# Two-layer encoder on one core: the low parts of the queries stored at full height per head, and the on-chip buffers shared out anew

## The chip, the cores and the metric

One core of one Trainium2 chip. The metric is device time in microseconds, the median of several runs. The engines are named as in the profile: PE is TensorE (its weight loads stand as PEld), DVE is VectorE, ACT is ScalarE, POOL is GpSimd, SP is SyncE, which here only issues DMAs.

## The reference

Two layers. Each has a SwiGLU feed-forward block, a mixer and a second feed-forward block, each behind an RMS norm whose shift, scale and gate come from a conditioning vector `c`. The mixer sums three gated branches: attention A with a relative-position bias, pooling B, and attention C with forget gates. 512 tokens, 1024 features, 8 heads of 64 features in each attention. Cut to what matters here:

```python
mod = (silu(c) @ w_ada[l] + b_ada[l]).reshape(B, 9, 1024)
h = modulate(rms_norm(x, norm_gain[l, 0]), mod[:, 0], mod[:, 1])
x = x + 0.5 * mod[:, 2] * swiglu(h, ffn_w_gate[l, 0], ffn_w_up[l, 0], ffn_w_down[l, 0])
h = modulate(rms_norm(x, norm_gain[l, 1]), mod[:, 3], mod[:, 4])
x = x + mod[:, 5] * hybrid_mixer(h, ...)     # two attentions, each:
#   logits = rms_norm(q, gq) * 64**-0.5 @ rms_norm(k, gk).T + bias;  softmax;  @ v
h = modulate(rms_norm(x, norm_gain[l, 2]), mod[:, 6], mod[:, 7])
x = x + 0.5 * mod[:, 8] * swiglu(h, ffn_w_gate[l, 1], ffn_w_up[l, 1], ffn_w_down[l, 1])
```

## The kernel before

**Three passes a product.** Activations lie feature-major: 128 features on partitions, the 512 tokens on the free axis. Every float32 operand of a large product is split into a high and a low float32r part, and a product is three matmuls: high by high, high by low, low by high (`triple`, L118 to L120). A weight chunk is 512 KB: `wchunk` (L221) has SP load it into a tile `raw`, ACT writes the high part `whi` (L246), and DVE, or POOL in attention A and C, writes the low part `wlo` as `raw` minus `whi` (L248). One chunk feeds 24 matmuls of 512 columns. There are three tiles each of `raw`, `whi` and `wlo`.

**Modulation.** The 144 columns of `mod` are made on DVE, not on PE: a step (`mod_step`, L178) loads 512 KB of `w_ada` and one DVE instruction (L182) multiplies it by silu(c) and sums it, with a tiny read of the sum behind it. 16 steps stand in the start of the first block; the other 128 come from a queue, `MOD_RATE` = 0.8 steps for each weight chunk in a feed-forward block (L229). Their tiles are the same three `raw` tiles that the weights use, so weights and `w_ada` alternate in them.

**Who sets the order.** The source is written in one order, with tasks put off by a count of PE work (`later`, `poll`). A list scheduler then orders each engine's instructions once, at build time: an instruction may go ahead of one written earlier if the earlier one's inputs or its tile are not there yet in the scheduler's own reckoning. On the chip each engine takes its instructions in that fixed order.

**Norm between blocks.** The norm of the next block runs in two halves of 256 tokens while the last products of the block still run: DVE adds up the squares (L298), PE sums over features (L310), DVE takes 1/sqrt by three Newton steps of tiny instructions (L312 and L254 to L262) and scales a diagonal (L315), PE spreads it (L329), and DVE, POOL and ACT make eight pieces each of `hhi` and `hlo` (L338 to L343). The first three weight chunks of the next block go to tiles that attention uses (`ptb`, `pta`), so that they are ready before the norm.

**Logits.** `proj_qk` (L613) makes queries and keys, and `turn` puts them feature-major, two heads to 128 rows. For each head, `b[:, odd, :]` holds the high part in the head's own 64 rows; the other 64 rows hold, for the queries, the high part again, and for the keys the low part. So the first logits matmul (L746, 128 rows) gives high by high plus high by low. The low part of the queries lies in a tile `lows` shared by two pairs of heads, and the second matmul (L747) takes 64 rows of it against the 64 rows of the keys' high part. There are 4 query tiles for each of 8 heads, two attentions, two layers: 128 pairs of such matmuls, with 128, 256, 384 and 512 columns. Between the logits of one head stand turned weights (L769), products with V (L791, L792) and, as filler, the products of other branches.

Of the kernel before, what the change touches and what calls it, by code (L numbers as in the profile page):

```python
"""Two layers of a chunk-causal hybrid encoder (macaron SwiGLU, two attentions, pooling), one core.

Activations are held feature-major: features on partitions, the 512 tokens on the free axis.
Every float32 operand of a large product is split exactly into two float32r parts (12 bits each);
a product is three float32r passes: high*high + high*low + low*high.
"""
# [16 lines left out]
P = 128  # L23
T = 512
# [16 lines left out]
def encoder_kernel(tc, xT, c, w_ada, b_ada, gains, w_gate, w_up, w_down, w_qkv, w_f, w_ubg,  # L41
# [15 lines left out]
    uid = [0]  # L57

# [13 lines left out]
    def blk(tag, dt=F32R):  # L72
        bufs = {"xv": 4, "v2": 4, "b": 15}[tag]
        return st([P, 2, T], dt, tag, bufs)
# [53 lines left out]
    silc = [st([P, D], F32, "b", 15)]  # L128
    sil_dram = dr.tile([1, D], F32, name="sil_dram")
    crow = st([1, D], F32, "b", 15)  # L130
# [47 lines left out]
    def mod_step(l, j, d, tag="raw"):  # L178
        raw = st([P, D], F32, tag, 2 if tag != "raw" else 3)
        nc.sync.dma_start(raw, w_ada[l, j, d])  # L180
        m = modc[:, l, j, d:d + 1]
        nc.vector.tensor_tensor_reduce(out=raw, in0=raw, in1=silc[0], scale=1.0, scalar=badac[:, l, j, d:d + 1],  # L182
                                       op0=ALU.mult, op1=ALU.add, accum_out=m)
        s, kind = divmod(j, 3)
        if kind == 1:
            g = gainc[:, l, s, d:d + 1]
            return nc.vector.scalar_tensor_tensor(apre[:, l, s, d:d + 1], m, 1.0, g, op0=ALU.add, op1=ALU.mult).ins
        if kind == 2:
            nc.vector.tensor_scalar(m, m, 0.5, None, op0=ALU.mult)
# [4 lines left out]

    def mod_pop():
        if mod_ptr[0] < len(mod_queue):
            mod_step(*mod_queue[mod_ptr[0]])
            mod_ptr[0] += 1
# [5 lines left out]
    MOD_RATE = 0.8  # L204
# [7 lines left out]
    @contextlib.contextmanager  # L212
    def behind(engine):
        """What is issued here goes behind the last piece of the norm on that engine."""
        if engine in gate:
            with tc.issue_after(gate[engine]):
                yield
        else:
            yield

    def wchunk(src, shape, side=True, spare=None, lo_eng=None):  # L221
        if lo_eng is None:
            lo_share[1] += 1
            lo_eng = nc.gpsimd if lo_share[0] and lo_share[1] % lo_share[0] == 0 else nc.vector
        if quiet[0] > 0:
            quiet[0] -= 1
            if quiet[0] == 0:
                gate.clear()
        elif side and in_ffn[0]:  # L229
            mod_credit[0] += MOD_RATE  # L230
            while mod_credit[0] >= 1.0:
                mod_credit[0] -= 1.0
                mod_pop()
        raw = st([P] + list(shape), F32, "raw", 3)
        nc.sync.dma_start(raw, src)
        if spare == "ptb":
            both = st([P, 2] + list(shape), F32R, "ptb", 2)
            hi, lo = both[:, 0], both[:, 1]
        elif spare == "pta":
            hi = st([P] + list(shape), F32R, "pta", 2)  # L240
            lo = st([P] + list(shape), F32R, "pta", 2)
        else:
            hi = st([P] + list(shape), F32R, "whi", 3)
            lo = st([P] + list(shape), F32R, "wlo", 3)
        with behind("scalar"):
            nc.scalar.copy(hi, raw)  # L246
        with behind("vector"):
            lo_eng.tensor_tensor(lo, raw, hi.bitcast(F32), op=ALU.subtract)  # L248
        return hi, lo

# [21 lines left out]
    class Norm:  # L272
        """sq() takes in the finished tiles of x, front() and back() make one half of hhi/hlo."""
# [9 lines left out]
        def sq(self, d, hs):  # L283
            """hs: 0 or 1 for a half, None for all tokens."""
            cols = slice(0, T) if hs is None else slice(hs * HALF, (hs + 1) * HALF)
            x = xd(d)[:, cols]
            n = cols.stop - cols.start
            if d == 0:
                nc.scalar.activation(self.ssum[:, cols], x, AF.Square)
            elif d < KD - 1:  # L290
                q = t1(T)[:, :n]
                nc.scalar.activation(q, x, AF.Square)  # L292
                nc.gpsimd.tensor_tensor(self.ssum[:, cols], self.ssum[:, cols], q, op=ALU.add)  # L293
            else:
                self.work[hs] = st([P, 3 * HALF], F32, "strip", 2)
                w = self.work[hs][:, :HALF]
                nc.scalar.activation(w, x, AF.Square)
                nc.vector.tensor_tensor(w, w, self.ssum[:, cols], op=ALU.add)  # L298
            if d % 2 == 0 and self.xa[d // 2] is None:
                self.xa[d // 2] = blk(self.xtag, F32)  # L300
            nc.scalar.activation(self.xa[d // 2][:, d % 2, cols], x, AF.Identity, scale=apre[:, self.l, self.s, d:d + 1])  # L301
# [54 lines left out]
    def k_outer(chunk_src, nch, lhs_rhs, before_last=None):  # L356
        """chunk_src(c) -> AP of two K-tiles; lhs_rhs(hi, lo, ktile, j) -> operands of tile j.

        Yields (tile, half, sums) as they finish; the halves of the tokens come apart only with before_last."""
# [36 lines left out]
    def residual_tail(d, hs, acc_j, gate, nxt):  # L396
        """x += gate * product, and what the next norm takes from it."""
# [15 lines left out]
    class Ffn:  # L413
# [11 lines left out]
        def prefetch_weights(self):  # L425
            self.pre = [self.gate_up(0, 0, spare="ptb"), self.gate_up(1, 0, spare="ptb"), self.gate_up(0, 1, spare="pta")]
# [15 lines left out]
        def run(self, nxt):  # L442
            l, s, ms = self.l, self.s, self.ms
            in_ffn[0] = True
            for part, (f0, nf) in enumerate(((0, 12), (12, 10))):
# [33 lines left out]
                for c0 in (0, T):  # L479
# [9 lines left out]
                    if last and c0 == 0 and nxt is not None:  # L489
                        nxt.prefetch("v2")  # L490
                    split = last and c0 > 0
# [10 lines left out]
        def start(self):  # L502
            """The first three units while the modulation that they need still arrives."""
# [9 lines left out]
            with behind("vector"):  # L513
                mod_step(l, 0, 0, "ptb")
# [13 lines left out]
            with behind("vector"):  # L528
                ready = [mod_step(l, 1, 0, "pta")]
            gate.clear()  # L530

            def h(d):
# [6 lines left out]
                if d + 1 < KD:  # L539
                    with tc.issue_after(ready[0]):  # L540
                        mod_step(l, 0, d + 1, "ptb")
                    with tc.issue_after(scaled):
                        ready[0] = mod_step(l, 1, d + 1, "pta")
# [69 lines left out]
    def proj_qk(l, col, gcol, is_q, res, pre=None, norm=None):  # L613
# [22 lines left out]
        def turn(p):  # L636
# [4 lines left out]
            b = blk("b")  # L641
            first, second = slice(0, HD), slice(HD, P)
            for odd, (own, other) in enumerate(((first, second), (second, first))):
# [4 lines left out]
                if is_q:  # L648
                    nc.scalar.activation(low, pt[own, :], AF.Identity, scale=gc)
                    if p % 2 == 0 and odd == 0:  # L650
                        lows.append(blk("b"))
                    low = lows[p // 2][own, p % 2, :]
                nc.vector.scalar_tensor_tensor(low, pt[own, :], gc, dst[own, :].bitcast(F32),
                                               op0=ALU.mult, op1=ALU.subtract)
            res.append((b, lows[p // 2][:, p % 2, :]) if is_q else b)
# [20 lines left out]
    def finish_turns(upto=3):  # L676
        """The turned queries and keys of the head pairs up to this one are needed from here on."""
# [56 lines left out]
    def attention(qs, ks, vs, strip, ys, filler, budget, group):  # L734
        """All heads; per query tile: logits and softmax, later the turned weights, later the product with V.
        Between them goes other work for TensorE (filler)."""
        open_pt = {}

        def logits(h, i, strips):
            p, off = divmod(h, 2)  # L740
            rows = slice(off * HD, off * HD + HD)
# [5 lines left out]
            mm(s[:, :n], ql[rows, i * P:(i + 1) * P], k[rows, odd, :n], start=False, stop=True)  # L747
# [13 lines left out]
        def turn(h, i, pr):  # L761
            half, c = divmod(i, 2)
            nj = 2 * half + 2
            if c == 0:
                open_pt[h] = st([P, 2, nj, 256], F32R, "ptb" if half else "pta", 2)
# [55 lines left out]
    def pool_front(l, g):  # L821
# [5 lines left out]
        u = st([P, T + 16], F32, "pta", 2)  # L827
# [28 lines left out]
    def wpool_load(l):  # L856
        raw = st([P, 4, P], F32, "t1", 2)
        nc.sync.dma_start(raw, w_pool[l].rearrange("g c e -> c g e"))
        w = st([P, 2, 4, P], F32R, "pta", 2)
# [39 lines left out]
    class Mixer:  # L899
# [7 lines left out]
        def prefetch_weights(self):  # L907
            self.pre = [qkv_chunk(self.l, 0, c, spare=t) for c, t in enumerate(("ptb", "ptb", "pta"))]

        def run(self, nxt):  # L910
# [54 lines left out]
            if l + 1 < L:  # L965
                silc[0] = st([P, D], F32, "b", 15)
# [99 lines left out]
```

## Time and profile before

| | us |
|---|---|
| median of three runs | 2517.68 (2516.93 to 2517.75) |
| the profiled execution: span from first to last instruction | 2516.3 |
| PE busy | 2473.2 (98%) |
| DVE busy | 1373.3 (55%) |
| ACT busy | 981.1 (39%) |
| POOL busy | 361.9 (14%) |

For the profiled execution its span is the time that is known; the median of the runs is 1.4 us above it. The busy share of PE counts a matmul from its start to its modelled end, and neighbours overlap, so how dense PE works is read from the distance between the starts of matmuls, not from the share. The page also names the idle time in front of a group of instructions and what ended it; "issue" there means that the engine waited for nothing that the profile shows.

### The profile page before, as it was taken

To read this page: it belongs to the slowest core of one execution; us is meant where nothing else is said; L and a number is where in the kernel's file an instruction comes from. 1 tells how busy PE (TensorE), PEld (TensorE's weight loads), DVE (VectorE), ACT (ScalarE), POOL (GpSimd) and SP (SyncE) were. 2 spreads that over 40 slices of the span, in tenths; PEclk is the share of its full clock that TensorE was granted. 3 is DMA by queue.
4 is the path that set the end of the run, shared out by engine and by line. 5 is a ranking of instruction groups with operands and counts; after the bars stand their busy time and mean duration, and the time that the engine had idled before them with its cause. 6 is when DMAs were issued, how large, how long until landed. Compare 5 with 4: busy or idle time off the path is not lost. (4 is left out here: it accounts for less than half of the span.)

```text
span 2516.3 us, 30919 instructions
## 1 busy us (share of the span) xinstructions
PE 2473.2 (98%) x11898; PEld 2037.0 (81%) x11898; DVE 1373.3 (55%) x2429; ACT 981.1 (39%) x1632; POOL 361.9 (14%) x337
## 2 busy tenths in 40 slices
PE   6999999999999999999999999999999999999999
PEld 4888888766788898888888888977777888888888
DVE  8645546678753465555465555476777434533332
ACT  4322235666542352223342222356765323422231
POOL 2000002333322120000020000123232322100000
PEclk9999999999999999999999999999999999999999
DMA  7555543222323435545425554322132233223222
GB/s 247 199 175 176 178 158 101 83 72 86 113 83 105 151 101 173 178 168 176 143 101 175 169 182 154 131 91 82 54 108 97 89 110 133 76 93 100 98 95 84
DMA packets 116263, 320.02 MB, mean 127 GB/s; under 512 B 11122, under 2 KB 13298, under 8 KB 116116
## 3 DMA queue, kind: packets, MB, share of 16 engines
q1 hardware_dynamic: 116114, 318.05, 37.5%
q8 instruction: 93, 1.52, 0.2%
q14 instruction: 54, 0.44, 0.0%
q10 hardware_dynamic: 2, 0.00, 0.0%
HBM read 311.64 MB, written 6.38 MB: 126 GB/s over the span
## 5 line engine op out<-in xcount | busy, mean ns | idle before, releaser
L246 ACT CAST whi<-raw 128x1024 fp32r<-128x1024 f32 (+1 forms) x395 | 411.3, 1045 | 1058.0 <-PE acc L119 420.1
L248 DVE TENSOR_TENSOR wlo<-raw,whi 128x1024 fp32r<-128x1024 f32 x339 | 417.2, 1234 | 380.7 <-ACT whi L246 372.2
L118 PE MATMUL mm<-hhi,whi 128*128 128x512 f32 x1304 | 507.6, 389 | 0.0
L119 PE MATMUL mm<-hlo,whi 128*128 128x512 f32 x1304 | 507.3, 389 | 0.0
L120 PE MATMUL mm<-hhi,wlo 128*128 128x512 f32 x1304 | 507.3, 389 | 0.0
L118 PE MATMUL acc<-b,whi 128*128 128x512 f32 (+1 forms) x960 | 356.9, 372 | 0.0
L119 PE MATMUL acc<-b,whi 128*128 128x512 f32 (+1 forms) x960 | 353.8, 369 | 0.0
L120 PE MATMUL acc<-b,wlo 128*128 128x512 f32 (+1 forms) x960 | 353.7, 368 | 0.0
L182 DVE CUSTOM_DVE_ANT_0 raw<-raw,b,badac 128x1024 f32<-128x1024 f32 x128 | 164.4, 1284 | 254.4 <-DMA raw<-in_w_ada_dram 254.1
L118 PEld LDWEIGHTS mm<-hhi,whi 128*128 128x128 f32 x1304 | 245.0, 188 | 50.7
L120 PEld LDWEIGHTS mm<-hhi,wlo 128*128 128x128 f32 x1304 | 244.7, 188 | 51.0
L119 PEld LDWEIGHTS mm<-hlo,whi 128*128 128x128 f32 x1304 | 244.8, 188 | 50.8
L120 PEld LDWEIGHTS acc<-b,wlo 128*128 128x128 f32 x960 | 180.9, 188 | 30.3 <-issue 0.4
L119 PEld LDWEIGHTS acc<-b,whi 128*128 128x128 f32 x960 | 181.0, 189 | 30.0 <-issue 0.9
L118 PEld LDWEIGHTS acc<-b,whi 128*128 128x128 f32 x960 | 180.9, 188 | 30.1
L293 POOL TENSOR_TENSOR ssum<-ssum,t 128x256 f32<-128x256 f32 (+1 forms) x45 | 48.8, 1084 | 1070.7 <-ACT t L292 1070.7
L118 PE MATMUL acc<-hhi,whi 128*128 128x512 f32 x480 | 194.0, 405 | 3.2 <-ACT hhi L536 3.2
L120 PE MATMUL acc<-hhi,wlo 128*128 128x512 f32 x480 | 189.8, 395 | 3.0 <-POOL wlo L248 3.0
L119 PE MATMUL acc<-hlo,whi 128*128 128x512 f32 x480 | 188.9, 394 | 1.5 <-DVE hlo L538 1.5
L248 POOL TENSOR_TENSOR wlo<-raw,whi 128x1024 fp32r<-128x1024 f32 (+1 forms) x56 | 133.4, 2386 | 198.9 <-ACT whi L246 170.5
L118 PE MATMUL acc<-whi,hhi 128*128 128x512 f32 x336 | 144.5, 430 | 2.9 <-ACT t L623 2.5
L437 DVE TENSOR_TENSOR t<-mm,t 128x512 f32<-128x512 f32 x86 | 59.4, 691 | 137.9 <-PE mm L120 136.2
(234 smaller groups left out, 3569.5 us busy)
## 6 DMA issues: line engine op xcount, KB each, us to landing
raw<-in_w_ada_dram SPq DMA_DIRECT2D x128, 512.0 KB, 4.3
raw<-in_w_down_dram SPq DMA_DIRECT2D x88, 512.0 KB, 3.7
raw<-in_w_gate_dram SPq DMA_DIRECT2D x85, 512.0 KB, 3.6
raw<-in_w_up_dram SPq DMA_DIRECT2D x85, 512.0 KB, 3.5
raw<-in_w_ubg_dram SPq DMA_DIRECT2D x56, 512.0 KB, 3.5
raw<-in_w_qkv_dram SPq DMA_DIRECT2D x48, 512.0 KB, 3.6
raw<-in_w_branch_dram SPq DMA_DIRECT2D x24, 512.0 KB, 3.7
raw<-in_w_out_dram SPq DMA_DIRECT2D x16, 512.0 KB, 4.3
```

Source lines behind the costliest of these rows:

```text
L118: mm(o, lh, rh, start=start, stop=False)
L119: mm(o, lh, rl, start=False, stop=False)
L120: mm(o, ll, rh, start=False, stop=stop)
L182: nc.vector.tensor_tensor_reduce(out=raw, in0=raw, in1=silc[0], scale=1.0, scalar=badac[:, l, j, d:d + 1], op0=ALU.mult, op1=ALU.add, accu ...
L246: nc.scalar.copy(hi, raw)
L248: lo_eng.tensor_tensor(lo, raw, hi.bitcast(F32), op=ALU.subtract)
L293: nc.gpsimd.tensor_tensor(self.ssum[:, cols], self.ssum[:, cols], q, op=ALU.add)
L437: nc.vector.tensor_tensor(pr, pu, sg, op=ALU.mult)
```

## The change

The low parts of the queries get a tile per pair of heads, laid out per head: `lows[p][:, odd, :]` holds the low part in the head's own rows, and POOL writes zeros in the other 64. The second logits matmul then takes all 128 rows of it against all 128 rows of the keys' tile; what it adds is zero times the keys' low part. This needs two more 4 KB tiles per attention, and the tiles are shared out anew:

- `b` has 17 tiles instead of 15, `raw` 2 instead of 3, `pta` 1 instead of 2.
- the third prefetched weight chunk and the pooling branch's `u` move from `pta` to `b`.
- modulation steps use the four `v2` tiles (in attention C these hold the values) and no longer `raw`: in the start, and in every feed-forward block until the next block's norm needs `v2` (`mod_tag`). After that point a block issues no more steps. `MOD_RATE` goes from 0.8 to 1.0.

```diff
+    NB, NRAW = 17, 2
-        bufs = {"xv": 4, "v2": 4, "b": 15}[tag]
+        bufs = {"xv": 4, "v2": 4, "b": NB}[tag]
...
     def mod_step(l, j, d, tag="raw"):
-        raw = st([P, D], F32, tag, 2 if tag != "raw" else 3)
+        raw = st([P, D], F32, tag, {"v2": 4, "raw": NRAW}[tag])
...
-            mod_step(*mod_queue[mod_ptr[0]])
+            mod_step(*mod_queue[mod_ptr[0]], mod_tag[0])
...
-    MOD_RATE = 0.8
+    MOD_RATE = 1.0
...
-        elif side and in_ffn[0]:
+        elif side and in_ffn[0] and mod_tag[0] == "v2":
...
-        raw = st([P] + list(shape), F32, "raw", 3)
+        raw = st([P] + list(shape), F32, "raw", NRAW)
...
-        elif spare == "pta":
-            hi = st([P] + list(shape), F32R, "pta", 2)
-            lo = st([P] + list(shape), F32R, "pta", 2)
+        elif spare == "b":
+            hi = st([P] + list(shape), F32R, "b", NB)
+            lo = st([P] + list(shape), F32R, "b", NB)
...
             in_ffn[0] = True
+            mod_tag[0] = "v2"
...
                         nxt.prefetch("v2")
+                        mod_tag[0] = "raw"
...
             b = blk("b")
+            if is_q:
+                lows.append(blk("b"))
...
-                    if p % 2 == 0 and odd == 0:
-                        lows.append(blk("b"))
-                    low = lows[p // 2][own, p % 2, :]
+                    nc.gpsimd.memset(lows[p][other, odd, :].bitcast(F32), 0.0)
+                    low = lows[p][own, odd, :]
...
-            mm(s[:, :n], ql[rows, i * P:(i + 1) * P], k[rows, odd, :n], start=False, stop=True)
+            mm(s[:, :n], ql[:, odd, i * P:(i + 1) * P], k[:, odd, :n], start=False, stop=True)
...
-                open_pt[h] = st([P, 2, nj, 256], F32R, "ptb" if half else "pta", 2)
+                open_pt[h] = st([P, 2, nj, 256], F32R, "ptb" if half else "pta", 2 if half else 1)
...
-        u = st([P, T + 16], F32, "pta", 2)
+        u = st([P, T + 16], F32, "b", NB)
```

Because the steps have tiles of their own, the scheduler places them elsewhere. All line numbers of the changed kernel below are one to five higher than before for the same instruction.

First place, the DMA queue of SP in the first feed-forward block, behind the start. `raw` is a weight chunk or, before, a modulation step (`in_w_ada`). Before:

```order
L235 DMA raw_481<-in_w_gate_dram 128x1024
L180 DMA raw_487<-in_w_ada_dram 128x1024
L235 DMA raw_491<-in_w_up_dram 128x1024
L685 DMA wf_4694<-in_w_f_dram 128x64
L180 DMA raw_554<-in_w_ada_dram 128x1024
L235 DMA raw_558<-in_w_gate_dram 128x1024
L180 DMA raw_564<-in_w_ada_dram 128x1024
L235 DMA raw_568<-in_w_up_dram 128x1024
```

Here there are three steps for four weight chunks. Now, a few rows further on in the same block:

```order
L181 DMA v_117_635<-in_w_ada_dram 128x1024
L181 DMA v_121_645<-in_w_ada_dram 128x1024
L238 DMA raw_572<-in_w_up_dram 128x1024
L238 DMA raw_639<-in_w_gate_dram 128x1024
L181 DMA v_130_712<-in_w_ada_dram 128x1024
L181 DMA v_134_722<-in_w_ada_dram 128x1024
L238 DMA raw_649<-in_w_up_dram 128x1024
L238 DMA raw_716<-in_w_gate_dram 128x1024
L181 DMA v_143_789<-in_w_ada_dram 128x1024
L181 DMA v_147_798<-in_w_ada_dram 128x1024
```

From here on the steps settle at five for every two weight chunks until the 49 of the first block are through, by the 24th weight chunk behind the start; then the block has none. Before they were spread over the block and the mixer behind it.

Second place, DVE between the first mixer and the second feed-forward block, in the second half of the norm: from the sum of squares (`nt_v`) through the Newton steps to the first piece of `hlo`. Before:

```order
L343 SCALAR_TENSOR_TENSOR hlo<-b_7580,modc,hhi 128x256
L312 TENSOR_SCALAR nt_v_7784<-acc_7781 128x2
L254 TENSOR_SCALAR nt_j_7786<-nt_v_7784 128x2
L260 TENSOR_TENSOR nt_q_7788<-nt_j_7786 128x2
L261 SCALAR_TENSOR_TENSOR nt_u_7789<-nt_q_7788,nt_v_7784 128x2
L262 SCALAR_TENSOR_TENSOR nt_z_7790<-nt_u_7789,nt_j_7786 128x2
```

Here nothing stands between the instructions of the norm. Now:

```order
L315 TENSOR_SCALAR nt_v_7812<-acc_7809 128x2
L183 ISA v_1709_8463,modc<-v_1709_8463,b_6195,badac 128x1024
L183 ISA modc 128x1
L257 TENSOR_SCALAR nt_j_7814<-nt_v_7812 128x2
L183 ISA v_1713_8472,modc<-v_1713_8472,b_6195,badac 128x1024
L183 ISA modc 128x1
L263 TENSOR_TENSOR nt_q_7816<-nt_j_7814 128x2
L183 ISA v_1722_8538,modc<-v_1722_8538,b_6195,badac 128x1024
L183 ISA modc 128x1
L264 SCALAR_TENSOR_TENSOR nt_u_7817<-nt_q_7816,nt_v_7812 128x2
L183 ISA v_1726_8547,modc<-v_1726_8547,b_6195,badac 128x1024
```

Nine modulation steps now stand on DVE between `nt_v` and the first piece of this half, two more between the half's sum of squares and `nt_v`, and four around the same chain of the first half. Before there were none in either chain. At the other norms no step stands in the chain, in either kernel.

More of the change, by code (lines that the diff above doesn't have):

```diff
@@ L127, in encoder_kernel @@
     nc.vector.memset(ones, 1.0)
-    silc = [st([P, D], F32, "b", 15)]
+    silc = [st([P, D], F32, "b", NB)]
     sil_dram = dr.tile([1, D], F32, name="sil_dram")
-    crow = st([1, D], F32, "b", 15)
+    crow = st([1, D], F32, "b", NB)
     nc.scalar.dma_start(crow, c)
@@ L193, in encoder_kernel @@
     mod_credit = [0.0]
+    mod_tag = ["v2"]
     def mod_pop():
         if mod_ptr[0] < len(mod_queue):
-            mod_step(*mod_queue[mod_ptr[0]])
+            mod_step(*mod_queue[mod_ptr[0]], mod_tag[0])
             mod_ptr[0] += 1
@@ L425, in prefetch_weights @@
         def prefetch_weights(self):
-            self.pre = [self.gate_up(0, 0, spare="ptb"), self.gate_up(1, 0, spare="ptb"), self.gate_up(0, 1, spare="pta")]
+            self.pre = [self.gate_up(0, 0, spare="ptb"), self.gate_up(1, 0, spare="ptb"), self.gate_up(0, 1, spare="b")]
         def unit(self, o, w, cols=slice(0, T), ks=range(KD)):
@@ L513, in start @@
             with behind("vector"):
-                mod_step(l, 0, 0, "ptb")
+                mod_step(l, 0, 0, "v2")
             v = st([P, NT], F32, "nt_v4", 1)
@@ L528, in start @@
             with behind("vector"):
-                ready = [mod_step(l, 1, 0, "pta")]
+                ready = [mod_step(l, 1, 0, "v2")]
             gate.clear()
@@ L540, in h @@
                     with tc.issue_after(ready[0]):
-                        mod_step(l, 0, d + 1, "ptb")
+                        mod_step(l, 0, d + 1, "v2")
                     with tc.issue_after(scaled):
-                        ready[0] = mod_step(l, 1, d + 1, "pta")
+                        ready[0] = mod_step(l, 1, d + 1, "v2")
             def product(d, w):
@@ L649, in turn @@
                     nc.scalar.activation(low, pt[own, :], AF.Identity, scale=gc)
-                    if p % 2 == 0 and odd == 0:
-                        lows.append(blk("b"))
-                    low = lows[p // 2][own, p % 2, :]
+                    nc.gpsimd.memset(lows[p][other, odd, :].bitcast(F32), 0.0)
+                    low = lows[p][own, odd, :]
                 nc.vector.scalar_tensor_tensor(low, pt[own, :], gc, dst[own, :].bitcast(F32),
                                                op0=ALU.mult, op1=ALU.subtract)
-            res.append((b, lows[p // 2][:, p % 2, :]) if is_q else b)
+            res.append((b, lows[p]) if is_q else b)
         todo = [lambda p=p: turn(p) for p in range(4)]
@@ L740, in logits @@
             p, off = divmod(h, 2)
-            rows = slice(off * HD, off * HD + HD)
             (q, ql), k = qs[p], ks[p]
@@ L858, in wpool_load @@
         nc.sync.dma_start(raw, w_pool[l].rearrange("g c e -> c g e"))
-        w = st([P, 2, 4, P], F32R, "pta", 2)
+        w = st([P, 2, 4, P], F32R, "pta", 1)
         split_to(w[:, 0], w[:, 1], raw)
@@ L907, in prefetch_weights @@
         def prefetch_weights(self):
-            self.pre = [qkv_chunk(self.l, 0, c, spare=t) for c, t in enumerate(("ptb", "ptb", "pta"))]
+            self.pre = [qkv_chunk(self.l, 0, c, spare=t) for c, t in enumerate(("ptb", "ptb", "b"))]
         def run(self, nxt):
@@ L965, in run @@
             if l + 1 < L:
-                silc[0] = st([P, D], F32, "b", 15)
+                silc[0] = st([P, D], F32, "b", NB)
                 nc.sync.dma_start(silc[0], sil_dram.broadcast_to([P, D]))
```

## The prediction

> **What bounds the kernel now.** I read the page's busy times first, then the idle times in front of PE's weight loads, then the timeline of PE around the logits matmuls.
>
> ```profile
> PE 2473.2 (98%) x11898; PEld 2037.0 (81%) x11898; DVE 1373.3 (55%) x2429; ACT 981.1 (39%) x1632; POOL 361.9 (14%) x337
> ...
> PEld mm L747 <- issue: 25.2, 98, 0.4
> ...
> L747 PEld LDWEIGHTS mm<-b,b x128: 182/183/285, 467.1 to 1940.5; 64*128 64x128 f32 x128
> ```
>
> PE is the bound: 98% busy, everything else far below. But one of its weight loads waits, with nothing that the profile could name, and that is the load of the 64-row logits matmul. The timeline shows the 256-column and the 512-column pair:
>
> ```profile
> 501.39 0.39 PE L120 MATMUL acc<-whi,hlo 128*128 128x512 f32 x1
> 501.62 0.28 PE L746 MATMUL mm<-b,b 128*128 128x256 f32 x1
> 501.83 0.39 PE L747 MATMUL mm<-b,b 64*128 64x256 f32 x1
> 501.83 0.18 PEld L747 LDWEIGHTS mm<-b,b 64*128 64x128 f32 x1 [0.25 <-issue]
> 502.15 0.19 PEld L118 LDWEIGHTS acc<-whi,hhi 128*128 128x128 f32 x1
> 502.15 0.50 PE L118 MATMUL acc<-whi,hhi 128*128 128x512 f32 x1
> 502.25 0.19 PEld L119 LDWEIGHTS acc<-wlo,hhi 128*128 128x128 f32 x1
> 502.48 0.39 PE L119 MATMUL acc<-wlo,hhi 128*128 128x512 f32 x1
> 502.71 0.40 PE L120 MATMUL acc<-whi,hlo 128*128 128x512 f32 x1
> ...
> 505.76 0.28 PE L791 MATMUL mm<-ptb,xv 128*128 128x256 f32 x1
> 505.88 0.28 PE L792 MATMUL mm<-ptb,xv 128*128 128x256 f32 x1
> ...
> 526.01 0.39 PE L746 MATMUL mm<-b,b 128*128 128x512 f32 x1
> 526.33 0.50 PE L747 MATMUL mm<-b,b 64*128 64x512 f32 x1
> 526.76 0.50 PE L118 MATMUL acc<-whi,hhi 128*128 128x512 f32 x1
> 527.10 0.40 PE L119 MATMUL acc<-wlo,hhi 128*128 128x512 f32 x1
> ```
>
> Read the starts, not the durations. Between full-height matmuls a 512-column one takes 0.23 (502.48 to 502.71) and a 256-column one 0.12 (505.76 to 505.88), and the next load starts while the matmul before still runs. The load of L747 starts only with its matmul, when L746 is nearly done, and the load of the L118 behind it does the same. From L746 to L119 that is 0.86 for 256 columns against 0.12 + 0.12 + 0.23 = 0.47, and 1.09 for 512 against 3 x 0.23 = 0.69: 0.39 and 0.40 lost at each pair.
>
> **Term 1: the full-height second matmul.** It has the same columns as before, so it takes no longer than its neighbours; what goes is the 0.4 us at 128 pairs, 51 us. All of it lies on PE, but PE is given it back only where the other engines keep up in the 240 us of each layer in which the pairs stand:
>
> ```profile
> 520.00:540.00 20.00, 19.60 (x99) 14.76 (x97) 15.41 (x42) 18.85 (x41) 2.54 (x2) 1.00 0.13 41
> 540.00:560.00 20.00, 17.19 (x66) 12.56 (x65) 16.35 (x36) 8.28 (x19) 10.27 (x6) 0.83 0.27 92
> ...
> 600.00:620.00 20.00, 19.46 (x105) 14.34 (x104) 16.86 (x57) 15.57 (x43) 6.31 (x10) 1.00 0.30 101
> ```
>
> The columns are PE, PEld, DVE, ACT, POOL, PE's clock and the DMA share. Six pairs in 20 us would make that stretch 17.6 us. DVE needs 16.9 in the third row and ACT 18.9 in the first, so some of it comes back as waits. I take 3 to 4 us a layer off: 51 - 7 = 44 us gained; ends 30 and 51. The 32 new zero fills lie on POOL, idle 86% of the time, ahead of the products they serve; the nearest rows are two fills:
>
> ```profile
> L720 POOL MEMSET strip<- 64x64 f32 x16 | 2.3, 144 | 41.3 <-DMA strip<-in_rel_dram 33.5 <-DVE qss L624 6.5 <-DVE t L796 1.3
> L687 POOL MEMSET ssum<- 128x320 f32 x2 | 0.7, 364 | 2.2 <-DVE strip L298 2.2
> ```
>
> Some 0.5 us each, 16 us of POOL, nothing on the path; on the path they would cost at most 16.
>
> **Term 2: modulation steps in the norm behind the first mixer.** Before, the second half of that norm ran like this on DVE, with PE's wait behind it:
>
> ```profile
> 909.63 0.41 DVE L298 TENSOR_TENSOR strip<-strip,ssum 128x256 f32<-128x256 f32 x1
> ...
> 910.74 0.16 DVE L312 TENSOR_SCALAR nt_v<-acc 128x2 f32<-128x2 f32 x1 [0.30 <-PE acc L310]
> ...
> 914.58 1.09 DVE L338 TENSOR_TENSOR b<-acc,b 128x256 f32<-128x256 f32 x3 [1.20 <-ACT strip L331]
> 915.94 4.71 DVE L343 SCALAR_TENSOR_TENSOR hlo<-b,modc,hhi 128x256 fp32r<-128x256 f32 x8 [0.28 <-ACT hhi L342]
> ...
> 916.36 0.51 PE L118 MATMUL mm<-hhi,ptb 128*128 128x256 f32 x2 [0.45 <-ACT hhi L342]
> ...
> L182 DVE CUSTOM_DVE_ANT_0 raw<-raw,b,badac 128x1024 f32<-128x1024 f32 x128 | 164.4, 1284 | 254.4 <-DMA raw<-in_w_ada_dram 254.1
> ```
>
> PE already waits 0.45 us for the first piece, so this chain has no slack. The change puts 11 steps between L298 and the first piece, 11 x 1.28 = 14 us, and four around the first half, 5 us less about 1 us of slack there. PE has only the 24 triples of the first half to bridge it (8 us, which the chain used up before too). So 14 + 4 = 18 us of waiting. On SP the same steps put 17 DMAs in a row ahead of the sixth weight chunk of that block; at DVE's 1.28 us a step they are issued within 22 us, and PE holds five chunks (27 us) and waits besides, so this costs nothing; without that cover it would be up to 22 us, inside the bad end of term 3. A long wait has a second price, which the stall near 546 us shows:
>
> ```profile
> 548.00:550.00 2.00, 1.10 (x4) 1.11 (x5) 1.97 (x8) 1.98 (x5) 0.76 (x1) 0.71 0.63 174
> 550.00:552.00 2.00, 2.00 (x6) 1.36 (x6) 2.00 (x2) 0.34 (x1) 2.00 (x3) 0.50 0.54 219
> 552.00:554.00 2.00, 2.00 (x6) 1.52 (x6) 1.74 (x6) 0.71 (x3) 2.00 (x1) 0.50 0.00 0
> 554.00:556.00 2.00, 2.00 (x9) 1.51 (x8) 1.33 (x3) 0.09 (x1) 0.77 (x2) 0.58 0.20 45
> ```
>
> The clock is lost for 2 x (0.29 + 0.50 + 0.50 + 0.42) = 3.4 us. Term 2 is +21; ends 8 (if most steps fall into waits that DVE has anyway) and 26 (if their DMAs come late as well).
>
> **Term 3: dense stretches in the feed-forward blocks.** Five steps per two chunks, and per two chunks PE takes 48 x 0.23 = 11.0 us. On DVE: 5 x 1.28 + 2 x 1.23 + 0.69 + 0.69 = 10.2 us, 93%, from L182 and these rows:
>
> ```profile
> L248 DVE TENSOR_TENSOR wlo<-raw,whi 128x1024 fp32r<-128x1024 f32 x339 | 417.2, 1234 | 380.7 <-ACT whi L246 372.2
> ...
> L353 DVE TENSOR_TENSOR b<-t,b 128x512 fp32r<-128x512 f32 x88 | 60.3, 685 | 2.1 <-ACT b L352 2.1
> L437 DVE TENSOR_TENSOR t<-mm,t 128x512 f32<-128x512 f32 x86 | 59.4, 691 | 137.9 <-PE mm L120 136.2 <-ACT t L435 1.5
> ...
> 30.00:40.00 10.00, 10.00 (x46) 8.26 (x45) 10.00 (x15) 3.87 (x6) 4.90 (x2) 1.00 0.87 304
> 160.00:180.00 20.00, 20.00 (x90) 16.57 (x89) 9.58 (x17) 4.76 (x5) 0.00 (x0) 1.00 0.55 184
> ```
>
> Seven transfers of 512 KB in 11.0 us are 334 GB/s. Such blocks moved 184 before, and the densest row moves 304 at a share of 0.87, so full use would be some 350. Both queues just fit. Three prepared chunks (16 us of PE work) cover a slip of 0.3 us a chunk over 18 chunks, except right behind the start, where little is prepared. I take +4; ends 0 and 25, the latter if 304 is all there is: 3.67 MB then take 12.1 us, 1.1 us more per pair, for some 23 pairs.
> By the Trainium skill, page "Perfetto Trace Analysis", section "Roofline", the 16 DMA engines of a core move about 435 GB/s together; that ceiling would leave a fifth free, term 3 would be 0 and the total 4 us less. No row here comes above 304, so I keep the row.
>
> **Term 4: two `raw` tiles.** In steady work a chunk's tile is needed again only after two chunks, 11.0 us, against load, split and subtract of some 6 us: nothing. At the five norms the third prefetched chunk now loads one tile later, and its subtraction stands in DVE's queue ahead of the last residual and the sum of squares. There each norm has no slack (above), so about 1 us each: +4, ends 0 and 10. `pta` with one tile and `b` with 17 for two more live: nothing, covered by the distance of a head's turn to its product; if that fails it shows inside attention and is in the low end of term 1.
>
> **Sum.** -44 + 21 + 4 + 4 = -15. The span of 2516.3 becomes 2501; the median lies 1.4 above the span, so 2517.7 - 15 = 2503.
>
> **Rivals.**
> (A) The steps are nearly free: DVE takes them in waits of its own, PE keeps what it wins. For it: DVE is 55% busy on the whole. Against it: the fixed order puts nine steps into a chain that PE waits for. -50 + 8 + 2 = -40: 2478. Chance 0.17.
> (B) Slower: the transfers saturate. Its place is the dense stretches. It decides from the point where fewer than 334 GB/s come through; SP then holds weight chunks behind steps whose tiles are not free, and PE runs out. Price 25, with 26 in the norm, 8 for `raw` and 41 gained: +18: 2536. For it: no row above 304. Against it: none of those rows was limited by transfers alone. Chance 0.12.
> (C) Slower too: the change doesn't do what it says, because a load still can't start under a matmul on the same rows. Then nothing is gained, and terms 2 to 4 stay: 2517.7 + 29 = 2547. Against it: in the rows above the load of L119 starts at 502.25 under the L118 that runs from 502.15 to 502.65, both on 128 rows, and the starts are 0.23 apart. Chance 0.04.
> The Trainium skill states a rule of that kind: page "TensorE: Matmul & The Clock Gate", section "Part 3: Packing small matmuls — row/col tiling", says that loads overlap with running matmuls only when the row groups differ. The trace shows the opposite at these rows.
> (D) Attention is held by DVE and ACT, and only 30 come back: 2517.7 - 30 + 29 = 2517. The rows at 520 and 540 speak for it, the other stretches against. Chance 0.07.
>
> **The numbers.** The forecast, 2503, has 0.60; its own ends, 2486 and 2516, are term 1 between 36 and 51 with term 2 between 12 and 25. 0.2% is 5 us, about what a measurement of this kernel can tell from no change. Faster by more: A and nine tenths of the forecast, 0.71. Within: D and the rest of the forecast, 0.12. Slower: B, C and a little of D, 0.17. The range 2475 to 2520 takes in A, D and the forecast and leaves out B and C.
>
> **What would show it.** After the change the starts from L746 on should be 0.06 to 0.23 apart with no "issue" idle before the second load. DVE should show L183 between the Newton steps at the first mixer's end, PE a wait of some 15 us there and the clock at 0.50 behind it. In the first 200 us DVE should be over 90% busy and DMA over 300 GB/s. I am wrong if PE waits in the feed-forward blocks, if that norm costs PE under 8 us, or if the attention stretches shrink by less than 15 us a layer.

## The result and the profile after

The changed kernel takes 2528.62 us (median of 4 runs, 2527.62 to 2537.46) against 2517.3 beside it: ratio 1.0054, 95% interval 1.0039 to 1.007. It is slower, by 11 us, and so is the profiled execution (span 2527.3 against 2516.3).

I cut all traces at the same matmuls, counted from the start, and took the time between their starts. The right-hand columns are experiments that come below.

| stretch, us | before | changed | e1 | e4 | e5 | e9 | e6 |
|---|---|---|---|---|---|---|---|
| norm before layer 1's mixer | 94.9 | 98.2 | 95.1 | 95.1 | 98.7 | 95.1 | 94.9 |
| attention, layer 1 | 257.7 | 245.2 | 244.3 | 257.0 | 257.3 | 250.4 | 236.5 |
| norm behind layer 1's mixer | 80.9 | 107.5 | 80.8 | 105.9 | 107.3 | 80.8 | 81.0 |
| norm between the layers | 75.8 | 78.0 | 75.8 | 75.8 | 79.7 | 75.8 | 75.8 |
| norm before layer 2's mixer | 94.9 | 96.8 | 95.0 | 95.1 | 97.7 | 95.1 | 95.2 |
| attention, layer 2 | 256.8 | 245.1 | 244.7 | 256.0 | 256.0 | 250.1 | 235.6 |
| norm behind layer 2's mixer | 80.8 | 82.3 | 80.8 | 80.9 | 85.0 | 80.8 | 81.0 |
| all the rest | 1571.4 | 1571.2 | 1571.4 | 1571.1 | 1572.9 | 1571.1 | 1571.4 |

So the attentions gained 24.2 us, the norm behind the first mixer lost 26.6, the other four norms lost 8.9, and the feed-forward blocks, with all their extra steps, did not move.

**Logits.** The timeline of PE in the changed kernel, a 256-column and a 512-column pair:

```profile
487.90 0.28 PE L751 MATMUL mm<-b,b 128*128 128x256 f32 x1
488.02 0.27 PE L752 MATMUL mm<-b,b 128*128 128x256 f32 x1
488.13 0.40 PE L119 MATMUL acc<-whi,hhi 128*128 128x512 f32 x1
488.36 0.39 PE L120 MATMUL acc<-wlo,hhi 128*128 128x512 f32 x1
...
494.57 0.40 PE L751 MATMUL mm<-b,b 128*128 128x512 f32 x1
494.80 0.40 PE L752 MATMUL mm<-b,b 128*128 128x512 f32 x1
495.04 0.39 PE L119 MATMUL acc<-whi,hhi 128*128 128x512 f32 x1
495.26 0.39 PE L120 MATMUL acc<-wlo,hhi 128*128 128x512 f32 x1
```

The starts are 0.12, 0.11 and 0.23 apart, and 0.23, 0.24 and 0.22: nothing is lost at these pairs any more. But PE now waits for others. Its waits in the first layer's attention (450 to 720 us), first five rows of before and then of after:

```profile
PE mm L792 <- DVE pta L774: 1.1, 1, 1.1
PE mm L746 <- DVE mx L750: 1.0, 2, 0.8
PE mm L769 <- DVE nt_z L262: 1.0, 1, 1.0
PE mm L791 <- ACT pta L773: 0.8, 1, 0.8
PE mm L769 <- DVE mx L750: 0.8, 1, 0.8
```

```profile
PE mm L774 <- DVE t L762: 2.9, 3, 2.1
PE mm L797 <- DVE ptb L779: 2.1, 2, 1.2
PE mm L751 <- DVE t L801: 1.9, 3, 1.1
PE mm L751 <- DVE mx L755: 1.3, 2, 1.0
PE mm L774 <- DVE nt_z L265: 1.2, 1, 1.2
```

All rows of that view together are 5.7 us before and 14.1 after, nearly all for DVE. From the starts of the matmuls the balance can be drawn for both layers. I took, for each matmul, the distance to the next start less 0.44 ns a column. Where this excess is under 0.4 us, the sum fell from 97.8 to 50.0 us, 48 us given back (0.37 a pair). Where it is over 0.4 us, it rose from 13.5 us (16 places) to 37.2 (42 places): 24 us taken again.

**The norm behind the first mixer.** PE's waits there (880 to 940 us), pieces of DVE's timeline, and the windows with PE's clock behind the five busy times:

```profile
PE mm L119 <- ACT hhi L345: 9.1, 2, 4.6
PE acc L332 <- DVE strip L318: 6.4, 1, 6.4
PE mm L313 <- DVE modc L190: 2.7, 1, 2.7
```

```profile
915.03 0.16 DVE L315 TENSOR_SCALAR nt_v<-acc 128x2 f32<-128x2 f32 x1 [1.37 <-PE acc L313]
915.11 1.28 DVE L183 CUSTOM_DVE_ANT_0 v<-v,b,badac 128x1024 f32<-128x1024 f32 x1
...
917.59 0.16 DVE L263 TENSOR_TENSOR nt_q<-nt_j 128x2 f32<-128x2 f32 x1
917.66 1.28 DVE L183 CUSTOM_DVE_ANT_0 v<-v,b,badac 128x1024 f32<-128x1024 f32 x1
...
928.50 0.42 DVE L341 TENSOR_TENSOR b<-acc,b 128x256 f32<-128x256 f32 x1
```

```profile
890.00:900.00 10.00, 7.28 (x36) 7.07 (x36) 7.54 (x21) 3.17 (x9) 2.79 (x3) 0.66 0.85 317
900.00:910.00 10.00, 4.97 (x27) 4.07 (x26) 8.51 (x20) 4.91 (x12) 5.60 (x7) 0.83 0.32 109
910.00:920.00 10.00, 9.62 (x69) 9.42 (x67) 8.63 (x20) 0.51 (x1) 0.00 (x0) 0.83 0.54 170
920.00:930.00 10.00, 1.22 (x2) 0.50 (x2) 8.47 (x25) 1.01 (x3) 2.25 (x3) 0.68 0.91 325
930.00:940.00 10.00, 8.21 (x47) 8.04 (x48) 9.44 (x19) 4.95 (x9) 2.35 (x3) 0.64 0.51 172
```

Between `nt_v` and the first piece, 13.5 us pass (3.8 before), a step of 1.28 us between one tiny instruction and the next. The named waits are 18.2 us. The clock, 1.00 here before, is lower in all five rows; I put the other 8 of the 26.6 down to it: in steps of half a microsecond, PE's busy time multiplied by the missing share of the clock adds up to 9.6 us between 880 and 950 us, and to nothing before.

**The dense stretches.** First block, same columns; the last two are the DMA share and GB/s:

```profile
80.00:100.00 20.00, 20.00 (x90) 16.57 (x89) 17.10 (x27) 6.13 (x8) 0.00 (x0) 1.00 0.94 333
100.00:120.00 20.00, 20.00 (x90) 16.58 (x89) 18.22 (x34) 6.14 (x8) 0.00 (x0) 1.00 0.86 309
120.00:140.00 20.00, 20.00 (x90) 16.57 (x89) 18.22 (x34) 5.40 (x7) 0.00 (x0) 1.00 0.96 355
```

DVE is busy for 86 to 91%, 355 GB/s come through, and PE does not wait.

### The profile page after: what moved, and what is told of

Same layout as the page of the kernel before. It is cut to its first block, busy times and chain, and to the rows that moved or that the text cites. A ratio compares the mean times of both kernels' runs of the same rounds, so it can differ in the third digit from the quotient of the medians.

```text
span 2527.3 us, 30875 instructions
## 1 busy us (share of the span) xinstructions
PE 2439.7 (97%) x11898; PEld 2037.1 (81%) x11898; DVE 1366.0 (54%) x2429; ACT 980.6 (39%) x1632; POOL 386.1 (15%) x369
## 5 line engine op out<-in xcount | busy, mean ns | idle before, releaser
L119 PEld LDWEIGHTS mm<-hhi,whi 128*128 128x128 f32 x1304 | 245.1, 188 | 50.8
L296 POOL TENSOR_TENSOR ssum<-ssum,t 128x256 f32<-128x256 f32 (+1 forms) x45 | 55.3, 1228 | 1085.9 <-ACT t L295 1085.9
L183 DVE CUSTOM_DVE_ANT_0 v<-v,b,badac 128x1024 f32<-128x1024 f32 x144 | 183.3, 1282 | 23.5 <-DMA v<-in_w_ada_dram 22.5
L119 PE MATMUL acc<-whi,hhi 128*128 128x512 f32 x336 | 138.2, 411 | 4.8 <-ACT t L628 3.7
```

What stands on the lines that cost most here:

```text
L119: mm(o, lh, rh, start=start, stop=False)
```

## Experiments

Theories after this reading. W: at the pairs the full-height matmul gives back what it promised, but about half returns as waits for DVE and ACT. B, its rival: the attention waits because of the buffers given away. N: the steps inside the first mixer's norm cost 26 us; its rivals put that on the two `raw` tiles.

**e1_shared.** From the kernel before:

```diff
-            mm(s[:, :n], ql[rows, i * P:(i + 1) * P], k[rows, odd, :n], start=False, stop=True)
+            mm(s[:, :n], ql[:, i * P:(i + 1) * P], k[:, odd, :n], start=False, stop=True)
```

> The kernel before with one edit: the second logits matmul takes all 128 rows of the shared tile of lows, in which the other head's lows stand in the other 64 rows. It adds the other head's query lows times this head's key lows, a product of two low parts that the three-pass scheme otherwise leaves out, of the size of float32 rounding. No tile, no zero fill and no modulation step moves. Theory W (the attention's distances were set for a slower PE, so most of what the second matmul gives back turns into waits for DVE and ACT): the two attentions shrink by 9 to 12 us a layer as they do in the changed kernel, 2517 - 21 = 2496. Theory B (the waits in the changed attention come from the buffers given away: one pta, two raw, 17 b with zero fills): the full 0.4 us at 128 pairs comes back, 2517 - 44 to 51 = 2466 to 2473. Between 2480 and 2488 both hold half.

2492.33 us; ratio to before 0.9901 (0.9887 to 0.9916). The attentions lose 13.4 and 12.1 us, as in the changed kernel, with every buffer as before. W holds and B falls: the waits come with the faster PE, not with the buffers.

**e2_half.** From the changed kernel:

```diff
-            mm(s[:, :n], ql[:, odd, i * P:(i + 1) * P], k[:, odd, :n], start=False, stop=True)
+            mm(s[:, :n], ql[rows, odd, i * P:(i + 1) * P], k[rows, odd, :n], start=False, stop=True)
```

> The changed kernel with the second logits matmul back on the head's own 64 rows (of the zero-padded tile); tiles, fills and steps stay as changed. Theory W: it loses about 21 us, 2528 + 21 = 2550, because the waits in attention go away again as PE is slower. Theory B: the waits of the buffers stay and the 0.4 us a pair comes on top of them, 2528 + 44 to 51 = 2572 to 2580. The waits for the first mixer's norm stay as they are (PE idle about 20 us between 889 and 931 us) under both.

2555.78 us; 1.0149 (1.0134 to 1.0164), 27 us more than the changed kernel. The two attentions account for 19.4 of it, the rest lies in the norms, which were not edited and vary by some us in every kernel with two `raw` tiles. W again.

**e3_held.** From the changed kernel; `last_lo` is the subtraction of the chunk before:

```diff
-                mod_pop()
+                with tc.issue_after(last_lo[0]):
+                    mod_pop()
```

> The changed kernel, but every queued modulation step may be issued only behind the low-part subtraction of the weight chunk that stands ahead of it, so that none is pulled into the norm behind the first mixer and there is one step a chunk. Theory N (the steps in that norm's chain cost what its stretch lost, 26 us with the clock): the waits at 889 to 931 us go, 2528 - 24 to 28 = 2500 to 2504. Rival (two raw tiles or the late weight chunk behind them hold that norm): the waits stay, 2520 to 2528.

2510.57 us; 0.9976 (0.9965 to 0.9986), its runs between 2504.5 and 2516.1. The norm behind the first mixer falls from 107.5 to 86.9 us, 20.6 of 26.6. So the steps do cost it; the forecast of 2500 to 2504 was still too good, since one wait stays, for the sum of squares:

```profile
PE mm L315 <- DVE strip L303: 3.0, 1, 3.0
```

**e4_steps.** From the kernel before, the steps alone moved:

```diff
-        raw = st([P, D], F32, tag, 2 if tag != "raw" else 3)
+        raw = st([P, D], F32, tag, {"v2": 4, "ptb": 2, "pta": 2}[tag])
...
-    MOD_RATE = 0.8
+    MOD_RATE = 1.0
...
-        elif side and in_ffn[0]:
+        elif side and in_ffn[0] and mod_tag[0] == "v2":
```

> The kernel before with the steps alone moved: they use the four v2 tiles, at a rate of 1.0, and stop when the next block's norm needs v2; raw keeps 3 tiles, b 15, pta 2, the second matmul 64 rows. Theory N: the steps pulled into the first mixer's norm cost 20 to 30 us, 2538 to 2547. Rival (they only cost together with two raw tiles): 2517 to 2522.

2542.37 us; 1.0102 (1.0087 to 1.0117), in the trace all of it in that norm: 105.9 us against 80.9. N holds. Both sides are now shown: moving the steps alone costs 25, taking them out of the norm gives back 18.

**e5_raw2.** From e4_steps:

```diff
-        raw = st([P] + list(shape), F32, "raw", 3)
+        raw = st([P] + list(shape), F32, "raw", 2)
```

> The kernel of the run e4_steps with one number changed: raw has 2 tiles instead of 3 (b 15, pta 2, 64-row second matmul, steps in v2 as there). e2_half differs from e4_steps in raw, pta, b and the zero fills together and took 13 us more, by the starts of matmuls nearly all of it at the five norms (5.6 us at the last, about 3 at the others) and none in attention. Theory R (the two raw tiles cost it): 2542 + 11 to 14 = 2553 to 2556. Rival (pta, b or the fills cost it): 2541 to 2545.

2557.59 us; 1.0158 (1.0143 to 1.0173): 15 us more than e4_steps, 15.6 in the five norms, the attentions unchanged. So two `raw` tiles cost 15 here, and `pta`, `b` and the fills nothing that shows in e2_half. The timeline of e5 in the last norm shows how, without PE:

```profile
2175.77 0.48 DVE L401 SCALAR_TENSOR_TENSOR xv<-mm,modc,xv 128x256 f32<-128x256 f32 x1
2175.88 0.33 SPq L236 DMA_DIRECT2D raw<-in_w_up_dram  x1
2177.04 1.05 ACT L247 CAST pta<-raw 128x1024 fp32r<-128x1024 f32 x1 [1.73 <-DMA raw<-in_w_gate_dram]
2177.99 0.41 ACT L293 ACTIVATE t<-xv 128x256 f32<-128x256 f32 x1
2178.12 1.23 DVE L249 TENSOR_TENSOR pta<-raw,pta 128x1024 fp32r<-128x1024 f32 x1 [1.87 <-ACT pta L247]
...
2179.26 0.48 DVE L401 SCALAR_TENSOR_TENSOR xv<-mm,modc,xv 128x256 f32<-128x256 f32 x1
2180.29 0.42 DVE L299 TENSOR_TENSOR strip<-strip,ssum 128x256 f32<-128x256 f32 x1 [0.55 <-ACT strip L298]
```

The third prefetched chunk arrives late; ACT waits 1.73 us for it, DVE 1.87 for ACT, and behind that subtraction stand the last residual and the sum of squares, for which PE waits.

**What holds DVE in attention.** One row of the changed kernel led on. Its timeline, a normalisation of 512 columns in the usual time and, 8 us later, the same instruction:

```profile
608.24 0.48 DVE L762 TENSOR_SCALAR t<-t,rs 128x512 f32<-128x512 f32 x1
...
616.41 2.34 POOL L251 TENSOR_TENSOR wlo<-raw,whi 128x1024 fp32r<-128x1024 f32 x1
...
616.57 2.47 DVE L762 TENSOR_SCALAR t<-t,rs 128x512 f32<-128x512 f32 x1
...
619.09 0.42 PEld L774 LDWEIGHTS mm<-ident,t 128*128 128x128 f32 x4 [2.58 <-DVE t L762]
```

DVE's instruction starts under POOL's subtraction and ends after it, and PE's next load waits 2.58 us. Of the 128 normalisations, 31 in the changed kernel, 26 in e1 and 23 before take over 0.15 us more than the shortest of their size, each with a POOL instruction beside it: 31, 27 and 21 us in all. Of the other 97 in the changed kernel, 11 have one beside them. The Trainium skill, page "SBUF — State Buffer", section "Who interferes with whom", states that VectorE and GpSimd share a port pair that the instruction which takes it first holds to its end. The rows agree: 0.48 us became 2.47.

**e6_pool4.** From e1_shared, inside attention only (`cut` is a quarter of the chunk):

```diff
-            lo_eng.tensor_tensor(lo, raw, hi.bitcast(F32), op=ALU.subtract)
+                for q in range(4):
+                    lo_eng.tensor_tensor(lo[cut], raw[cut], hi[cut].bitcast(F32), op=ALU.subtract)
```

> The kernel of the run e1_shared, with POOL's subtraction of the low part in the two attentions cut into four instructions of a quarter each. In e1_shared 26 of the 128 normalisations on DVE (L757) take up to 2.7 us in place of 0.28 to 0.49, each while such a subtraction of 2.4 us runs on POOL: 27 us in all. Theory L (one instruction on POOL holds DVE's till it ends, and these delays feed the waits in attention): the excess falls to some 10 us and the time by 5 to 12, 2480 to 2487. Rival (the waits come from the distances alone): within 3 us of 2492. A bad side is POOL itself, if four instructions take far longer than one: over 2495.

2478.98 us; 0.9848 (0.9832 to 0.9865): 13 us less than e1_shared. The group of normalisations, in e1 and in e6:

```profile
L757 DVE TENSOR_SCALAR t<-t,rs 128x128 f32<-128x128 f32 (+3 forms) x128 | 76.0, 594 | 3.3
```

```profile
L764 DVE TENSOR_SCALAR t<-t,rs 128x128 f32<-128x128 f32 (+3 forms) x128 | 60.9, 475 | 3.3
L253 POOL TENSOR_TENSOR wlo<-raw,whi 128x256 fp32r<-128x256 f32 x192 | 140.9, 766 | 125.6 <-ACT whi L246 83.2 <-PE mm L799 25.0 <-PE acc L119 17.3
```

The excess falls from 27 to 11 us although POOL works longer (4 x 0.77 for 2.4). Theory L holds, with a little more than the 5 to 12 us forecast. The cut also changes the order on all engines, so this run alone doesn't tie the 13 us to the shorter hold; e9 and e10 below repeat the gain in two other kernels.

**e7_far.** From e1_shared: `LAG_T, LAG_V = 24, 14` becomes `30, 18`.

> The kernel of the run e1_shared with longer distances in attention: turned weights 30 instead of 24 passes behind their logits, products with V 18 instead of 14 behind those. Theory D (the distances, counted in PE work, are now too short in time): 5 to 15 us less, 2477 to 2487. Rival (three tiles of t2 and the load of DVE hold attention, not the distance): 2489 to 2500, since the logits then wait for tiles.

2498.71 us; 0.9926 (0.9911 to 0.9941): 6 us slower than e1_shared. Theory D falls.

**e8_act.** From e1_shared:

```diff
-            nc.vector.tensor_scalar(pr, pr, rs, None, op0=ALU.mult)
+            nc.scalar.activation(pr, pr, AF.Identity, scale=rs)
```

> The kernel of the run e1_shared with the normalisation of the softmax weights on ACT instead of DVE: 128 instructions, some 36 us a layer with what POOL adds to them, leave DVE (busy 202 of 260 us there), and some 32 us a layer come to ACT (172 of 260). Theory L and that of DVE's load: attention gains 5 to 15 us, 2477 to 2487. Rival (ACT, which then is at 204 of 260 us, takes DVE's place): 2490 to 2505.

2500.2 us; 0.9931 (0.9917 to 0.9946): 8 us slower, in the rival's range. ACT is now busy for 199 of the 260 us and DVE for 171. The largest row of PE's waits is now for ACT (3.8 us), but those for DVE together are still 11 us, so that ACT takes DVE's place is shown only in part.

**e9_before_pool4, e10_after_pool4.** The cut of e6 in the kernel before and in the changed one.

> The kernel before with only POOL's subtraction cut into four, as in e6_pool4; the second logits matmul on 64 rows. Theory X (the delays that POOL puts on DVE cost time only once PE is faster; the 64-row pairs hid them): 2513 to 2517. Rival (they cost the same whatever the logits matmul does): as much as from e1_shared to e6_pool4, 13 us, 2502 to 2506. Under theory X the full-height matmul is worth some 36 us when nothing holds DVE, under the rival still 25.

2506.38 us; 0.9949 (0.9937 to 0.9962): 12 us less. My theory X fell: POOL's hold costs nearly the same with 64 rows. So it is an old cost of this kernel, and explains only some 3 us of what the full-height matmul failed to bring: that is worth 24.6 us with it and 27.4 without (e9 to e6), a difference that these runs barely resolve. Counted by the distances between matmuls as above, the full-height matmul gives back 42 us without the hold (48 with it), and 13 are taken again in gaps over 0.4 us (24 with it).

> The changed kernel with only POOL's subtraction cut into four. If the delays that POOL puts on DVE (31 us on its normalisations, 27 in e1_shared) took back part of what the full-height matmul gained here too: 2528 - 12 to 18 = 2510 to 2516, all of it in the two attentions. If something else of the change holds its attention (one pta, the fills): 2524 to 2530.

2514.66 us; 0.9985 (0.9976 to 0.9994), 14 us less than the changed kernel, as forecast; the attentions fall from 245.2 and 245.1 to 237.5 and 237.2.

**e11_pool8, e12_pool4_v18.** From e6_pool4: eight pieces instead of four; and `LAG_V` 18 instead of 14.

> e6_pool4 with eight instructions of an eighth in place of four. If the length of one POOL instruction is what counts: 2 to 5 us less, 2474 to 2477. If POOL's longer total (four pieces already take 3.06 us against 2.42) counts more, or what is left is no longer this: 2478 to 2486.

2472.16 us; 0.9814 (0.9801 to 0.9828). The best kernel of this study, 46 us faster than before and 56 faster than the changed one. It is 7 us less than e6, more than forecast, while the excess on the normalisations falls only from 11 to 10 us; where these 7 us come from is not shown.

> e6_pool4 with the products with V 18 instead of 14 passes behind their turned weights (the distance of the turned weights stays 24). The longest wait left in its attention is 2.4 us at 540 us and its twin in the second layer, a product with V that waits for the low part of its turned weights. If the distance to those products is what is short: 3 to 8 us less, 2471 to 2476. If not: 2477 to 2482.

2490.22 us; 0.9887 (0.9874 to 0.9901), 11 us slower than e6_pool4 and outside both forecasts.

**e13_near, e14_fill, e15_act_q.** From e11_pool8: `LAG_T` 20; `FILL_A, FILL_C` 10.5, 10.0; the normalisation of query tile 0 on ACT.

> e11_pool8 with turned weights 20 instead of 24 passes behind their logits. Longer distances made it slower twice (e7_far, e12). If the waits left in attention (some 8 us a layer in gaps over 0.4 us) come from work that the distances push together, a shorter one takes 3 to 8 us off: 2464 to 2469. If the distance was the right one and is now short in time: slower, 2475 to 2490.

2489.36 us; 0.9888 (0.9874 to 0.9903): 17 us slower than e11.

> e11_pool8 with a tenth more filler work between the query tiles (10.5 and 10.0 passes instead of 9.5 and 9.0), which gives back in time what the faster pairs took out of it. If DVE and ACT are too short of time for each query tile: 3 to 6 us less, 2466 to 2469. If the filler then runs out and the last heads stand without it: slower, 2474 to 2480.

2487.62 us; 0.988 (0.9863 to 0.9896): 15 us slower than e11, more than even the bad side had it.

> e11_pool8 with a quarter of the normalisations (the first query tile of each head, 32 instructions of 128 columns) on ACT: DVE loses some 6 us a layer, ACT gains some 6. If DVE's load makes the waits that are left: 2 to 5 us less, 2467 to 2470. If ACT is as late as DVE: 2472 to 2478.

2474.91 us; 0.9833 (0.9818 to 0.9847): 3 us slower. Three misses: no distance, filler or load that I tried beats the values the kernel has. Each also changes the order on all engines; how much of the 15 and 17 us is due to that was not separated. What makes the waits that are left with eight pieces (17 us in the two attentions) stays open.

## Why the prediction was wrong

**Term 1 is the step that failed:** "I take 3 to 4 us a layer off: 51 - 7 = 44 us gained; ends 30 and 51". The mechanism was right, and the 51 nearly so: 48 us came back at the pairs and around them. The part that returns as waits was mis-sized: 24 us, 12 a layer, not 3 to 4. So 24 us net, below the lower end, in e1 too, where nothing else was changed. The sign of being wrong that the prediction named for it was met: the attentions shrank by 12.5 and 11.7 us, less than 15 a layer. I had set busy times against a shortened 20 us and found DVE at 16.9 of 17.6 in one row and ACT at 18.9 in another; the 3 to 4 us follow from neither. Busy times leave out the order. In the changed kernel between 440 and 700 us, nearly all of the first attention, DVE is busy for 200 of the 260 us; it waits 18.0 us for ACT's exponentials, and ACT waits 29.8 us for DVE's maxima (20.3 and 30.1 before). I read this as a chain in which an engine can be late at single places while it is far from full. Before, the slow pairs had hidden part of this: gaps over 0.4 us at 16 places became 42. That the waits come with the faster PE is shown by e1 and e2; what makes each place late is argued, not shown. Rival D said that DVE and ACT hold the attention and priced the gain at 30, with a chance of 0.07.

**Term 2 was right in place and a few us too cheap:** 26.6 us against +21, just past its upper end of 26; with the steps alone (e4) it was 25.0. The waits were 18.2 against 18, but that they agree so well is luck: 10.9 in the second half instead of 14, 7.3 in the first instead of 4. The clock took some 9 us, not the 3.4 that I had read from one stall; here there were four waits. e3 and e4 show the cause from both sides.

**Term 3 was 0, not +4.** The extra steps of the feed-forward blocks are free. By the Trainium skill, page "Perfetto Trace Analysis", section "Roofline", full use is about 435 GB/s, and the forecast named 0 as what follows from it. The rows do not contradict it: 355 over 20 us, and PE does not wait. I had taken 304 as if it could be the limit, but the kernel before already moved 386 GB/s from 5 to 15 us, a stretch that my rows had split in two (290 and 305). Rival B falls with it.

**Term 4 was too small:** +4, ends 0 and 10; 8.9 at four norms of the changed kernel, 16 and 17 at the same four in e10 and e2, which were not edited there, and 15.6 at five in e5. The chain was the one I had described; I had given it 1 us a norm where it takes 1.5 to 6. That `pta` and `b` cost nothing held, and the zero fills took 0.53 us each, as estimated.

**The sum:** -24 + 27 + 0 + 9 = +12 instead of -15. Of the 27 us between them, term 1 makes 20. (The forecast's own upper end, 2516, adds up to 2515 from its terms.) Rival C, that nothing is gained, fell with the starts at 488 us; rival A with term 2.

## What to carry to other kernels

When a change gives time back to the engine that bounds a kernel, look at that stage for the places where the other engines already arrive just in time; their average load does not show how many of these become waits. When a queue of background work gets buffers of its own, look where the scheduler will let it run, above all in the short serial chains between stages. A long GpSimd instruction beside a chain on VectorE is worth trying in pieces, even if the pieces take longer together.

## What the runs showed of the hardware

A logits matmul of 64 rows between matmuls of 128 rows cost 0.37 us a pair more than one of full height with the same columns (48 us at 128 pairs, before against changed). POOL's subtraction (2.4 us) held DVE's normalisation from 0.48 to 2.47 us, and cutting it brought 12, 13 and 14 us in three kernels, whatever the logits did. Four pieces take 0.77 us each, eight take 0.48, and eight were still 7 us faster than four. In the first mixer's norm PE waited 2.7, 4.6, 6.4 and 4.5 us, and in windows of 2 us the granted clock stood at 0.50 from 894 to 898, from 908 to 912 and from 924 to 936 us. The dense feed-forward stretches took 355 GB/s without a wait of PE.
